# Low-rank weight loads on GpSimd's queue, and rotary halves swapped by ScalarE copies, in a two-layer hybrid encoder

## The chip, the cores and the metric

The kernel runs on one core of one Trainium2 chip. The metric is the device time of one execution in microseconds (us), as the median of several runs. The engines are TensorE (PE; its weight loads are shown as PEld), VectorE (DVE), ScalarE (ACT), GpSimd (POOL) and SyncE (SP). Each engine executes its instructions in order; where one waits, all behind it on that engine wait too. Transfers are issued by the queue of an engine (here always SP before the change) and carried by the core's 16 DMA engines.

## The reference

Two layers, on x of 256 tokens by 2048 channels in float32. Cut to what matters here:

```
for l in range(2):
    h = rms_norm(x, norm_g[l])
    proj = h @ w_in[l]                       # r, k, v, xw, xa | g_rw | q, k_at, v_at, g_at
    r, k, v, xw, xa = bidir_token_shift(...) # neighbours mixed in, xw and xa have 96 columns
    # group A, 16 heads of 64, one scan per direction d:
    w = -softplus(-(w0[d] + tanh(xw) @ decay_up[d])) - 0.5      # low rank: 96 -> 1024
    a = sigmoid(a0[d] + xa @ iclr_up[d])                        # low rank: 96 -> 1024
    y_rw = wkv_scan(...) both directions, normed, plus bonus * v
    # group B, 16 query heads on 4 key heads of 64, window of 128:
    q, k_at = rope(q), rope(k_at)            # t1*cos - t2*sin, t2*cos + t1*sin on halves of 32
    y_at = softmax over the band, with a sink logit, times v_at
    x = x + concat(y_rw * silu(g_rw), y_at * silu(g_at)) @ w_out[l]
out = rms_norm(x) * final_g
```

## The kernel before

Everything is held transposed: channels on the 128 partitions, the 256 tokens along the free dimension. A projection tile is 128 output columns. It is computed in one PSUM tile `pm` (two of them in rotation) by 16 steps over the 2048 input channels, and each step is three matmuls (lines 269 to 271): weights and activations are each split into a rounded part (`hi`, `XH`) and a rest (`lo`, `XL`), and hi*hi, hi*rest and rest*hi are added up.

The weights come as half tiles of 512 KB: `wload` (line 203) issues the load from SP into one of three `raw` buffers, and `wsplit` (lines 211 and 212) makes `hi` on ACT and `lo` on DVE, in two pieces of 512 columns each; two buffers of hi and lo are in rotation. The class `Stream` hands out the steps of all projections in a fixed order and starts a split one half tile ahead.

PE's order of work is written out by hand: the function `window` deals out 64 steps of projection in 14 slots and lets the generators of the scan (`scan_p`, `scan_i`, `scan_b`) or of the attention (`attend`) advance between slots. So the group A projections of head pair p run while earlier pairs are being scanned. The instructions of all other engines and queues are put in order by a scheduler that lists what is ready in its own estimate of time, by priority; this order is then fixed.

Per layer the projection order is: the two tiles of xw and xa; for each of 8 head pairs the tiles k, v, r and gate; v of the attention; two tiles of attention keys; eight of queries and eight of gates. The output projection has 16 tiles.

The places that the change touches:

- `ups` (lines 449 to 455), called at the first step of a pair's k tile. It loads the pair's columns of iclr_up (`iup`, 96 partitions of 2 x 128 numbers, tile `iu`) and of decay_up with the bias row w0 (`dup`, 97 partitions, tile `du`) into the two buffers of tag "g". The same two buffers serve the gate's `silu_evac` (lines 403 to 407), so a pair's loads wait until line 407 of the pair before.
- `value_evac` (line 457), one tile later, splits both into hi and rest: line 436 on ACT (`iuh`, `duh`), line 437 on DVE. `scan_p` uses them in matmuls (lines 617 to 619).
- `rope_evac` (lines 478 to 497), at the end of each of the two key tiles and eight query tiles of a layer. It copies `pm` to `raw` (tag "u") on ACT (line 487), loads `raw` into `rot` (tag "rrot") with neighbouring blocks of 32 partitions swapped, by four transfers from SP (line 489), and then multiplies and adds on DVE (lines 490 to 492); lines 494 and 495 split the result.
- POOL computes only the inverse square roots of norms: line 872 in `scan_b`, once per head pair, and line 190, once per layer and at the end.

Of the kernel before, what the change touches and what calls it, by code (L numbers as in the profile page):

```python
# [15 lines left out]
AF = mybir.ActivationFunctionType  # L16
ALU = mybir.AluOpType
# [111 lines left out]
def hybrid_trunk_kernel(ctx, tc, xT, wi, wv, wo, par, fing, dup, iup, sink, pos, cst, out):  # L129
    nc = tc.nc  # L130
    V, A, G, PE, SY = nc.vector, nc.scalar, nc.gpsimd, nc.tensor, nc.sync
# [18 lines left out]
    def st(tag, shape, dt=F32, bufs=1):  # L150
        return sp.tile([128, *shape], dt, tag=tag, name=tag, bufs=bufs)
# [230 lines left out]
    def queue_inputs(l):  # L382
# [66 lines left out]
        def ups(p, t):  # L449
            def begin():  # L450
                for n, src, rows in (("iu", iup, RANK), ("du", dup, RANK + 1)):
                    t[n] = st("g", [2, 128], bufs=2)
                    SY.dma_start(out=t[n][0:rows], in_=src[l, :, :, p * 128 : (p + 1) * 128].rearrange("d r c -> r d c"))

            return begin

# [21 lines left out]
        def rope_evac(place):  # L478
            def evac(pm):
                if not rope:  # L480
                    rope.extend((st("TW", [T]), st("XA", [T])))
                    V.tensor_tensor(rope[0], COS, L.norm.rb, op=ALU.mult)
                    V.tensor_tensor(rope[1], SIN, L.norm.rb, op=ALU.mult)
                CR, SR = rope
                raw = st("u", [T], bufs=2)
                rot = st("rrot", [T])
                A.activation(raw, pm, AF.Copy)
                for q in range(4):
                    SY.dma_start(out=rot[q * 32 : q * 32 + 32, :], in_=raw[(q ^ 1) * 32 : (q ^ 1) * 32 + 32, :])
                V.tensor_tensor(raw, raw, CR, op=ALU.mult)  # L490
                V.tensor_tensor(rot, rot, SR, op=ALU.mult)
                V.tensor_tensor(raw, raw, rot, op=ALU.add)
                hi, lo = place()
                A.activation(hi, raw, AF.Copy)
                V.tensor_tensor(lo, raw, hi.bitcast(F32), op=ALU.subtract)

            return evac
# [602 lines left out]
```

## Time and profile before

| | us |
|---|---|
| median of 3 runs | 1258.41 (1256.91 to 1259.39) |
| the profiled execution | 1254.45 |
| its span, first to last instruction | 1252.7 |
| PE busy | 1202.7 (96%) |
| PE weight load busy | 1126.2 (90%) |
| DVE busy | 947.1 (76%) |
| ACT busy | 735.6 (59%) |
| POOL busy | 18.5 (1%) |

The granted clock of TensorE, as a mean over the span, was 0.993 of full speed. Layer 0 runs to about 640 us, layer 1 after it.

How to read the rows. In the order of time a row is: start in us, duration in us, engine, line of the kernel, operation, output <- inputs by the program's names, count, and in brackets the time that the engine stood idle before it and what ended the idling. "SPq" is SP's queue, and L453 on it a DMA issue of line 453; several issues in a row are merged. A row of the waits is: who waited, for whom, then us in total, how many times, the longest. A row of a group is: line, engine, operation, shapes, count, busy us and mean ns of one. A row of the windows is: from:to, length, busy us of PE, PEld, DVE, ACT and POOL with instruction counts, granted clock of PE, mean share of the 16 DMA engines that was busy, GB/s.

### The profile page before, as it was taken

Reading aid. Unit: us, or ns where it says so; the run is one execution under the profiler, and the core shown is the slowest. Engines: PE = TensorE matmul, PEld = TensorE weight load, DVE = VectorE, ACT = ScalarE, POOL = GpSimd, SP = SyncE. Lnnn points to the kernel's source line nnn. Section 1 sums busy time; section 2 is a strip of 40 time slices with the busy share of each in tenths; the row PEclk is TensorE's granted clock in tenths of the full one; section 3 lists DMA queues with packets and bytes.
Section 4 is the critical chain, followed back from the end, with each engine's and each line's share of the span. In section 5 each row is a group of like instructions: output and inputs, shape, how many; then the busy total and the mean of one; then the engine's idle time right before and its main releaser. Section 6 shows DMA issues by size and latency. Waiting matters only on the chain.

```text
span 1252.7 us, 37475 instructions
## 1 busy us (share of the span) xinstructions
PE 1202.7 (96%) x15852; PEld 1126.2 (90%) x15852; DVE 947.1 (76%) x2113; ACT 735.6 (59%) x1838; POOL 18.5 (1%) x23
## 2 busy tenths in 40 slices
PE   7979999999999999999998999999999999999996
PEld 6979899999998988999998889999999888899996
DVE  7888878887886678856677878877887766786554
ACT  6655665665565466645555655665665555666553
POOL 0000000000000000000000000000000000000000
PEclk9999999999999999999999999999999999999998
DMA  6543223332323434366654333223322333345653
GB/s 245 163 136 120 92 92 122 100 96 95 120 86 96 131 109 144 123 219 230 210 188 142 126 125 103 92 92 125 103 92 86 116 108 129 126 143 168 213 192 119
DMA packets 60408, 166.67 MB, mean 133 GB/s; under 512 B 7728, under 2 KB 22736, under 8 KB 60240
## 3 DMA queue, kind: packets, MB, share of 16 engines
q1 hardware_dynamic: 60240, 164.27, 39.6%
q8 instruction: 124, 2.03, 0.7%
q14 instruction: 44, 0.36, 0.1%
HBM read 157.43 MB, written 4.19 MB: 129 GB/s over the span
## 4 chain that ended last, share of the span: by engine, by line
PE 66%; issue 15%; DVE 8%; ACT 6%; DMA 3%; SPq 1%; POOL 0%; POOLq 0%; DVEq 0%; ACTq 0%
PE pm L269 16%; PE pm L271 14%; PE pm L270 13%; PE pq L785 3%; PE pg L706 2%; DMA g<-dup 2%; DVE lo L212 2%; PE pd L796 2%; ACT suv L744 2%; PE pcc L831 2%; ACT AB L750 2%; PE pd L798 1%; PE py L840 1%; PE pcc L845 1%; ACT bt L739 1%
## 5 line engine op out<-in xcount | busy, mean ns | idle before, releaser
L269 PE MATMUL pm<-XH,hi 128*128 128x256 f32 x1664 | 499.9, 300 | 11.1 <-ACT XH L174 5.7
L211 ACT ACTIVATE hi<-raw 128x512 fp32r<-128x512 f32 x560 | 327.0, 623 | 272.6 <-PE pm L270 211.9
L271 PE MATMUL pm<-XH,lo 128*128 128x256 f32 x1664 | 470.5, 283 | 11.2 <-DVE lo L212 11.2
L270 PE MATMUL pm<-XL,hi 128*128 128x256 f32 x1664 | 469.6, 282 | 0.0
L212 DVE TENSOR_TENSOR lo<-raw,hi 128x512 fp32r<-128x512 f32 x560 | 369.7, 687 | 77.5 <-ACT hi L211 68.9
L269 PEld LDWEIGHTS pm<-XH,hi 128*128 128x128 f32 x1664 | 315.8, 190 | 24.8 <-ACT XH L174 6.0
L271 PEld LDWEIGHTS pm<-XH,lo 128*128 128x128 f32 x1664 | 316.0, 190 | 14.3 <-DVE lo L212 14.3
L270 PEld LDWEIGHTS pm<-XL,hi 128*128 128x128 f32 x1664 | 316.4, 190 | 1.5 <-DVE XL L175 0.7
L269 PE MATMUL pm<-MH,hi 128*128 128x256 f32 x512 | 144.5, 282 | 1.7 <-ACT hi L211 1.7
L271 PE MATMUL pm<-MH,lo 128*128 128x256 f32 x512 | 144.4, 282 | 0.4 <-DVE lo L212 0.4
L270 PE MATMUL pm<-ML,hi 128*128 128x256 f32 x512 | 144.1, 282 | 0.0
L269 PEld LDWEIGHTS pm<-MH,hi 128*128 128x128 f32 x512 | 97.1, 190 | 2.6 <-ACT hi L211 1.9
L271 PEld LDWEIGHTS pm<-MH,lo 128*128 128x128 f32 x512 | 97.1, 190 | 0.6 <-DVE lo L212 0.6
L270 PEld LDWEIGHTS pm<-ML,hi 128*128 128x128 f32 x512 | 97.2, 190 | 0.0
L785 PE MATMUL pq<-tv,AB 64*64 64x32 f16 x1536 | 43.8, 182 | 12.6 <-ACT AB L750 12.6
L850 ACT ACTIVATE suv<-pcc 64x128 f32<-64x128 f32 x128 | 34.4, 268 | 35.0 <-PE pcc L845 33.4
L785 PEld LDWEIGHTS <-AB 64*64 64x64 f16 x1536 | 34.4, 109 | 20.5 <-ACT AB L750 14.1
L752 DVE TENSOR_TENSOR AL<-ge,AB 64x512 f16<-64x512 f32 x32 | 22.0, 686 | 36.2 <-ACT AB L750 34.8
L799 DVE CAST_PREDICATED tv<-LV,pd 128x256 f16<-128x256 uint8 x80 | 34.4, 430 | 19.7 <-PE pd L798 18.8
L713 DVE TENSOR_TENSOR ge<-pg,C 128x512 f32<-128x512 f32 x64 | 41.3, 684 | 9.4 <-PE pg L706 9.4
L926 ACT ACTIVATE mv<-mv,mx 128x257 f32<-128x257 f32 x64 | 31.9, 500 | 23.2 <-DVE mx L923 23.2
L706 PE MATMUL pg<-mv,bk 64*128 64x128 f32 x512 | 37.2, 285 | 0.0
(230 smaller groups left out, 1863.9 us busy)
## 6 DMA issues: line engine op xcount, KB each, us to landing
raw<-wi SPq DMA_DIRECT2D x207, 512.0 KB
raw<-wo SPq DMA_DIRECT2D x64, 512.0 KB
raw<-wv SPq DMA_DIRECT2D x8, 512.0 KB
rrot<-u SPq DMA_DIRECT2D x80, 32.0 KB
vg<-xT SPq DMA_DIRECT2D x16, 128.0 KB
xd<-vg SPq DMA_DIRECT2D x16, 128.0 KB
vg<-xd SPq DMA_DIRECT2D x16, 128.0 KB
g<-dup SPq DMA_DIRECT2D x16, 97.0 KB
```

The lines of the kernel that those rows point to most:

```text
L211: A.activation(hi[:, q], raw[:, q], AF.Copy)
L212: V.tensor_tensor(lo[:, q], raw[:, q], hi[:, q].bitcast(F32), op=ALU.subtract)
L269: PE.matmul(pm, wh, rh[:, kk, :], start=(kk == 0), stop=False)
L270: PE.matmul(pm, wh, rl[:, kk, :], start=False, stop=False)
L271: PE.matmul(pm, wl, rh[:, kk, :], start=False, stop=(kk == 15))
L706: PE.matmul(pgs[h][:, c * 128 : (c + 1) * 128], BK[half[h], d, c, 1 - h : 3 - h, :].rearrange("p s j -> p (s j)"), MV[half[h], d, c].rearr ...
L713: V.tensor_tensor(GE[h][:, d].rearrange("p c s j -> p c (s j)"), pgs[h].rearrange("p (c x) -> p c x", c=NC), gm[d].unsqueeze(1).to_broadca ...
L744: A.activation(pick(SUV, half[1 - h], q * 128 + h * 64, [NC * 128, 2], [256, 2], [1, 64]), pts[h][half[q], 384:512].rearrange("p (b x) -> ...
L785: PE.matmul(narrow(pq, d, c, h), hq(AB, d, c, h), sub(TC, d, c, h, d * b), start=True, stop=True)
L799: V.copy_predicated(t_sub(TC), t_mask, flat4(pd))
L850: A.activation(here(h), pc[half[h], 1], AF.Copy)
L926: A.activation(Sc[:, h, q, 0:257], Sc[:, h, q, 0:257], AF.Exp, scale=0.125, bias=mx[:, q : q + 1], accum_out=den[:, q : q + 1])
```

## The change

It has two parts. The loads of the low-rank weights are issued from GpSimd's queue instead of SP's. And the swapped halves for the rotation are made by four ScalarE copies of 32 partitions each, straight from PSUM, instead of one ScalarE copy and four transfers; the first product on VectorE then reads PSUM too.

```
             def begin():
                 for n, src, rows in (("iu", iup, RANK), ("du", dup, RANK + 1)):
                     t[n] = st("g", [2, 128], bufs=2)
-                    SY.dma_start(out=t[n][0:rows], in_=src[l, :, :, p * 128 : (p + 1) * 128].rearrange("d r c -> r d c"))
+                    G.dma_start(out=t[n][0:rows], in_=src[l, :, :, p * 128 : (p + 1) * 128].rearrange("d r c -> r d c"))
...
                 raw = st("u", [T], bufs=2)
                 rot = st("rrot", [T])
-                A.activation(raw, pm, AF.Copy)
                 for q in range(4):
-                    SY.dma_start(out=rot[q * 32 : q * 32 + 32, :], in_=raw[(q ^ 1) * 32 : (q ^ 1) * 32 + 32, :])
-                V.tensor_tensor(raw, raw, CR, op=ALU.mult)
+                    A.activation(rot[q * 32 : q * 32 + 32, :], pm[(q ^ 1) * 32 : (q ^ 1) * 32 + 32, :], AF.Copy)
+                V.tensor_tensor(raw, pm, CR, op=ALU.mult)
                 V.tensor_tensor(rot, rot, SR, op=ALU.mult)
                 V.tensor_tensor(raw, raw, rot, op=ALU.add)
```

More of the change, by code (lines that the diff above doesn't have):

```diff
@@ L452, in begin @@
                     t[n] = st("g", [2, 128], bufs=2)
-                    SY.dma_start(out=t[n][0:rows], in_=src[l, :, :, p * 128 : (p + 1) * 128].rearrange("d r c -> r d c"))
+                    G.dma_start(out=t[n][0:rows], in_=src[l, :, :, p * 128 : (p + 1) * 128].rearrange("d r c -> r d c"))
             return begin
@@ L486, in evac @@
                 rot = st("rrot", [T])
-                A.activation(raw, pm, AF.Copy)
                 for q in range(4):
-                    SY.dma_start(out=rot[q * 32 : q * 32 + 32, :], in_=raw[(q ^ 1) * 32 : (q ^ 1) * 32 + 32, :])
-                V.tensor_tensor(raw, raw, CR, op=ALU.mult)
+                    A.activation(rot[q * 32 : q * 32 + 32, :], pm[(q ^ 1) * 32 : (q ^ 1) * 32 + 32, :], AF.Copy)
+                V.tensor_tensor(raw, pm, CR, op=ALU.mult)
                 V.tensor_tensor(rot, rot, SR, op=ALU.mult)
```

## The prediction

> **What bounds it now.** I read the page first (busy shares), then the idle gaps in PE's order of time, then the chain of waits, then the rows of the engines that PE waited for.
>
> ```profile
> span 1252.7 us, 37475 instructions
> PE 1202.7 (96%) x15852; PEld 1126.2 (90%) x15852; DVE 947.1 (76%) x2113; ACT 735.6 (59%) x1838; POOL 18.5 (1%) x23
> ```
>
> PE is busy 96% of the span, with a fixed amount of matmul, so only its 50 us of idle time, and stretches at a lower granted clock, can be won. PE's order of time shows where it idles; in brackets stand the idle time and what ended it.
>
> ```profile
> 65.49 0.38 PE L269 MATMUL pm<-XH,hi 128*128 128x256 f32 x1 [1.97 <-ACT hi L211]
> 69.52 0.38 PE L271 MATMUL pm<-XH,lo 128*128 128x256 f32 x1 [1.56 <-DVE lo L212]
> 75.51 0.39 PE L271 MATMUL pm<-XH,lo 128*128 128x256 f32 x1 [1.51 <-DVE lo L212]
> ...
> 352.31 0.42 PE L785 MATMUL pq<-tv,AB 64*64 64x32 f16 x15 [0.39 <-ACT AB L750]
> 398.79 0.61 PE L785 MATMUL pq<-tv,AB 64*64 64x32 f16 x15 [2.34 <-ACT AB L750]
> ...
> 558.55 0.38 PE L269 MATMUL pm<-MH,hi 128*128 128x256 f32 x1 [1.66 <-ACT hi L211]
> 559.43 0.58 PE L271 MATMUL pm<-MH,lo 128*128 128x256 f32 x1 [0.37 <-DVE lo L212]
> 678.54 0.38 PE L269 MATMUL pm<-XH,hi 128*128 128x256 f32 x1 [1.36 <-ACT hi L211]
> 682.57 0.39 PE L271 MATMUL pm<-XH,lo 128*128 128x256 f32 x1 [1.57 <-DVE lo L212]
> 688.56 0.38 PE L271 MATMUL pm<-XH,lo 128*128 128x256 f32 x1 [1.45 <-DVE lo L212]
> 1001.01 0.34 PE L811 MATMUL pn<-tt,q 64*64 64x64 f16 x10 [0.91 <-DVE q L807]
> 1010.94 0.42 PE L785 MATMUL pq<-tv,AB 64*64 64x32 f16 x15 [1.03 <-ACT AB L750]
> ```
>
> Three groups (65 to 76, 558, 678 to 689) wait for the weight split (hi on ACT, lo on DVE). A fourth (398.79, 1001 and 1010) is a scan step; in a pair without rotation the same wait is 0.39 (352.31). The question is what held ACT and DVE. The waits give it, then their rows at those places:
>
> ```profile
> ACT duh L436 <- DMA g<-dup: 10.4, 4, 4.4
> DVE u L490 <- DMA rrot<-u: 9.8, 11, 2.1
> ```
>
> ```profile
> 56.89 0.30 SPq L453 DMA_DIRECT2D g<-dup  x1
> 64.50 0.42 ACT L436 ACTIVATE duh<-g 97x256 fp32r<-97x256 f32 x1 [2.21 <-DMA g<-dup]
> 549.23 0.42 SPq L453 DMA_DIRECT2D g<-iup  x1
> 549.69 0.38 SPq L453 DMA_DIRECT2D g<-dup  x1
> 552.75 0.42 ACT L436 ACTIVATE iuh<-g 96x256 fp32r<-96x256 f32 x1 [0.42 <-DMA g<-iup]
> 557.57 0.42 ACT L436 ACTIVATE duh<-g 97x256 fp32r<-97x256 f32 x1 [4.40 <-DMA g<-dup]
> 669.54 0.30 SPq L453 DMA_DIRECT2D g<-dup  x1
> 677.55 0.42 ACT L436 ACTIVATE duh<-g 97x256 fp32r<-97x256 f32 x1 [2.57 <-DMA g<-dup]
> ```
>
> Each of the three groups follows an ACT that stands, in order, at duh until dup has landed: 7.6, 7.9 and 8.0 us after its issue. The split of the next weights is queued behind it. iup, a partition smaller, landed in 3.5 (549.23 to 552.75). The windows say why dup is late, and what an idle PE costs on top:
>
> ```profile
> 90.50:93.50 3.00, 1.50 (x25) 1.24 (x24) 0.87 (x2) 2.92 (x7) 0.00 (x0) 1.00 0.07 22
> ...
> 398.00:404.00 6.00, 5.21 (x60) 4.86 (x61) 4.33 (x10) 4.44 (x10) 0.00 (x0) 0.72 0.00 0
> 558.00:564.00 6.00, 5.08 (x28) 4.87 (x29) 4.14 (x9) 3.13 (x7) 0.00 (x0) 0.72 0.64 202
> ```
>
> From 90.5 to 93.5, with a dup in flight, the DMA share is 0.07, about one engine of 16, at 22 GB/s: its 97 KB crawl through one engine. After two of the PE gaps the granted clock averages 0.72 over 6 us: (1 - 0.72) x 6 = 1.7 us lost at each.
>
> **The change, part by part: the low-rank loads.** 32 issues (16 iup, 16 dup) leave SP, whose weight loads then no longer queue behind them, and go to POOL's queue. They still wait for the release of the two "g" buffers, so their issue time hardly moves. What queues behind them on POOL is the power of the scan's norm (and the layer's):
>
> ```profile
> 169.33 0.29 DVE L768 COPY tt<-EYE 128x512 f16<-128x512 f16 x1
> 169.82 0.30 SPq L453 DMA_DIRECT2D g<-dup  x1
> 180.48 0.41 ACT L436 ACTIVATE duh<-g 97x256 fp32r<-97x256 f32 x1
> 205.64 1.01 POOL L872 TENSOR_TENSOR yv<-yv,mhalf 128x4 f32<-128x4 f32 x1 [42.95 <-DVE yv L871]
> ```
>
> The power comes 36 us after the pair's loads and POOL idles 42.95 before it: cost nothing. In such a settled pair dup has 180.48 - 169.82 = 10.7 us until it is asked for, so a faster landing gains nothing there; the gain lies at the three places above.
>
> No row shows a load on POOL's queue. Bounds of dup's landing: 3.5 us (iup, 549.23), if it spreads over the engines; 8.0 (669.54), if it doesn't; above that only if POOL is slow to make it. It no longer stands behind weight loads in one queue, but POOL takes 1.01 us even for 128x4 elements, and iup goes first. I take 3.5 + 2 x 1.0 = 5.5, nearer the iup row, since dup differs from it by one partition. That is 2.1 (56.89), 2.4 (549.69) and 2.5 us (669.54) earlier.
>
> The rule for this is in the Trainium skill, DMA: Bandwidth & Descriptors, "Why a DMA increments its semaphore by 16 and not by 1": the engines used are the largest number up to 16 that divides the slowest dimension, which for 97 partitions is one. The 0.07 agrees. It names an exception: from GpSimd some plain copies use all 16, with the partitions dealt out. No run yet shows whether this load is one; with the exception the sum is mine, without it rival A.
>
> - Layer 0, second pair: PE's gaps are 1.97 + 1.56 + 1.51 = 5.0. ACT is released 2.1 us earlier; DVE, saturated after it, gets that time too. Gain 2.1 (0 to 5.0).
> - Layer 0, output projection: 1.66 + 0.37 of gap and 1.7 of clock. ACT's wait of 4.40 shrinks to 2.0, and 2.4 us earlier covers both gaps, so the clock has no reason to fall. Gain 3.7 (0 to 3.7).
> - Layer 1, second pair: gaps of 1.36 + 1.57 + 1.45 = 4.4, ACT released 2.5 earlier. Gain 2.4 (0 to 4.4).
> - Kernel start: the first pair's loads wait for nothing and may go out beside the first loads of x.
>
> ```profile
> 6.00:14.00 8.00, 6.64 (x24) 5.29 (x24) 6.78 (x17) 7.49 (x18) 0.00 (x0) 1.00 1.00 371
> 29.19 0.42 ACT L436 ACTIVATE duh<-g 97x256 fp32r<-97x256 f32 x1 [1.26 <-DMA g<-dup]
> ```
>
> At 371 GB/s their 193 KB push x back by 0.5; a wait of 1.26 goes. I count 0 (0.5 lost to 1.3 won).
>
> **The rotation.** Per tile of q or k: out go one ACT copy, four SP issues, four transfers; in come four ACT copies of 32 partitions from PSUM. VectorE's first product then reads PSUM.
>
> ```profile
> 387.55 0.37 ACT L487 ACTIVATE u<-pm 128x256 f32<-128x256 f32 x1
> 387.94 3.80 SPq L489 DMA_DIRECT2D rrot<-u  x4
> 393.15 0.43 DVE L490 TENSOR_TENSOR u<-u,TW 128x256 f32<-128x256 f32 x1 [2.09 <-DMA rrot<-u]
> ...
> L744 ACT ACTIVATE suv<-pt 64x256 f32<-64x256 f32 x64 | 24.2, 379 | 0.7
> L487 ACT ACTIVATE u<-pm 128x256 f32<-128x256 f32 x20 | 7.4, 369 | 0.1
> L394 DVE TENSOR_TENSOR u<-pm,rb 128x256 f32<-128x256 f32 x52 | 21.4, 414 | 9.8 <-PE pm L271 9.8
> ...
> 430.00:520.00 90.00, 88.81 (x907) 80.91 (x906) 70.36 (x216) 57.02 (x169) 1.01 (x1) 1.00 0.40 132
> ```
>
> From the ACT copy to DVE's product it now takes 5.6 us, and DVE, in order, stands idle 2.09 of it; the scan's work is queued behind. Half the partitions (L744) cost 379 ns where 128 cost 369, so 32 will not be cheaper: 4 x 0.38 - 0.37 = 1.15 us more of ACT per tile, 23 us in 20 tiles; latency falls to about 1.6 us. The product from PSUM costs what it did: 0.43 now (393.15), and the token shift reads pm at 414 ns (L394). pm is held some 2 us longer, until DVE has read it too; the next tile's 48 matmuls go to the other bank and, at the page's mean of 1202.7 / 15852 = 0.076 us, which the small ones pull down, take 3.6 or more. If that cover were gone, PE would wait for those 2. SP loses 80 issues, 3.80 us at each tile, and its weight loads start that much sooner; no PE gap above ends with such a load, so it counts 0.
>
> - Layer 0, second k tile: gap 2.34 back to 0.39 (1.95), and 1.7 of clock. Gain 3.6 (0 to 3.6).
> - Layer 1, same place: 0.91, and 1.03 back to 0.39. I take 1.4 of the 1.55.
> - The 16 q tiles: ACT is 57.0 of 90 us busy between 430 and 520, so most of the 1.15 lies beside other work; but the copies come just when the next split is due. I take 0.15 each of 0 to 1.15: loss 2.4 (0 to 18.4).
>
> **Sum:** 2.1 + 3.7 + 2.4 + 3.6 + 1.4 - 2.4 = 10.8 us won. The profiled execution took 1254.45 (span 1252.7), 4.0 under the median 1258.41; from the former 1243.7, on the scale of the median 1258.4 - 10.8 = 1247.6.
>
> **Rivals.** About 2.5 us (0.2%) is what a measurement here tells from no change.
>
> A. dup stays on one engine, and lands as late as now. Left is the rotation: 3.6 + 1.4 - 2.4 = 2.6, so 1255.8. For it: 0.07 now. Against: iup's 3.5 in the same form. The page's general rule speaks for it.
>
> B. ScalarE becomes late in the attention stage: 0.6 us shown per q tile, 9.6 in all instead of 2.4. Won remain 3.6, so 1254.8. For it: the split's queue; against: ACT's idle third.
>
> C. Slower: POOL makes the descriptors so slowly that dup lands later than today. Place: the same three waits of ACT. Each us beyond 7.9 costs 3; with 2.6 won by the rotation it decides (2.5 us slower) from a landing of 7.9 + 5.1 / 3 = 9.6 us. At 10.7, where the settled pairs begin to wait too, it is 3 x 2.8 - 2.6 = 5.8 slower: 1264.2. For it: 1.01 us for 512 elements on POOL. Against: nothing else runs there. The Trainium skill, SBUF — State Buffer, "SBUF: two separate sides", speaks for C: GpSimd can't write descriptors while VectorE runs a two-port copy. By the rows such a copy (L768) stands beside the issue, but it lasts 0.29 us, and is over 0.2 us before 169.82.
>
> **Chances.** My forecast 0.60, A 0.14, B 0.13, C 0.09, a reordering of ACT or DVE that costs more than all this 0.04. Faster by over 0.2%: 0.59 + 0.08 of A + 0.09 of B = 0.76. Within: 0.01 + 0.06 + 0.03 = 0.10, slower 0.01 + 0.09 + 0.04 = 0.14. The range: all upper bounds give 5.0 + 3.7 + 4.4 + 3.6 + 1.55 + 1.3 = 19.5, so 1239; up to 1259 it takes in A and B and leaves out C and the reordering.
>
> **What would show it.** Right: dup's transfer spread over the engines (no stretch at a DMA share of 0.07), ACT's wait for dup near zero, no clock of 0.72 after the output projection's start or the second k tile, no wait of L490 for a DMA. Wrong: duh waiting for DMA longer than 10.4 us in sum (C), or as long (A); PE waiting for the split after each group of four copies (B); PE gaps that move elsewhere.

## The result, and the profile after

The changed kernel took 1288.81 us in the median of 4 runs (1287.32 to 1289.56), beside 1257.66 for the kernel before on the same chip: a ratio of 1.0245, 95% interval 1.0228 to 1.0263. It is 31 us slower. The forecast was 10.8 us faster, and 1288.8 lies far above the range. In the profiled execution the changed kernel took 1288.49 us, 34.0 more than the 1254.45 of before.

The page of the kernel after, its first lines and its lines on the two loads (kind, count, KB each, median us from issue to landing):

```profile
span 1286.7 us, 37383 instructions
PE 1211.9 (94%) x15852; PEld 1134.9 (88%) x15852; DVE 947.7 (74%) x2113; ACT 761.6 (59%) x1898; POOL 76.0 (6%) x55
...
g<-dup POOLq DMA_DIRECT2D x16, 97.0 KB, 9.4
g<-iup POOLq DMA_DIRECT2D x16, 96.0 KB, 3.2
```

PE's idle time, span less busy, went from 50.0 to 74.8 us; the other 9.2 us of the longer span are PE busy for longer with the same 15852 matmuls. So two things are to be found: 24.8 us in which PE waited, and 9.2 us in which the same matmuls took longer. iup lands after 3.2 us, much as it did (3.5 in the prediction's rows); dup, one partition larger, in 9.4. The waits, and the groups of the two issues on POOL, show who felt it:

```profile
ACT duh L436 <- DMA g<-dup: 37.9, 4, 12.3
DVE u L489 <- ACT rrot L488: 15.3, 20, 1.5
```

```profile
L453 POOL DMA_DIRECT2D g<-dup x16 | 46.4, 2902 | 0.9
L453 POOL DMA_DIRECT2D g<-iup x16 | 10.8, 676 | 337.1 <-DVE vg L407 336.2 <-POOLq L1091 0.9
```

ACT's wait for dup is 37.9 us where it was 10.4. Issuing dup holds POOL for 2.90 us each time, issuing iup for 0.68. (From the rotation on, the line numbers of the changed kernel are lower by one.) A window with a dup in flight, the last three columns being granted clock, DMA share and GB/s:

```profile
76.00:79.00 3.00, 0.52 (x5) 0.31 (x3) 0.00 (x0) 0.00 (x0) 0.00 (x0) 1.00 0.09 23
```

The DMA share is 0.09, little over one engine of 16, as it was before. PE's order of time after shows where that reached PE:

```profile
19.04 0.58 PE L269 MATMUL pm<-XH,hi 128*128 128x256 f32 x1 [19.04 <-ACT XH L174]
...
82.33 0.58 PE L269 MATMUL pm<-XH,hi 128*128 128x256 f32 x1 [5.81 <-ACT hi L211]
83.68 0.58 PE L271 MATMUL pm<-XH,lo 128*128 128x256 f32 x1 [0.55 <-DVE lo L212]
86.98 0.58 PE L271 MATMUL pm<-XH,lo 128*128 128x256 f32 x1 [0.37 <-DVE lo L212]
93.80 0.38 PE L271 MATMUL pm<-XH,lo 128*128 128x256 f32 x1 [1.04 <-DVE lo L212]
...
571.05 0.56 PE L269 MATMUL pm<-MH,hi 128*128 128x256 f32 x1 [5.11 <-ACT hi L211]
705.82 0.58 PE L269 MATMUL pm<-XH,hi 128*128 128x256 f32 x1 [5.15 <-ACT hi L211]
707.17 0.58 PE L271 MATMUL pm<-XH,lo 128*128 128x256 f32 x1 [0.55 <-DVE lo L212]
710.47 0.58 PE L271 MATMUL pm<-XH,lo 128*128 128x256 f32 x1 [0.37 <-DVE lo L212]
716.50 0.38 PE L271 MATMUL pm<-XH,lo 128*128 128x256 f32 x1 [1.23 <-DVE lo L212]
```

The same three places as before, each with a first gap of over 5 us where it was 1.4 to 2.0, and a new one: the very first matmul comes at 19.04 us. Before, it came here:

```profile
5.72 0.58 PE L269 MATMUL pm<-XH,hi 128*128 128x256 f32 x1 [5.72 <-ACT XH L174]
```

So of the 24.8 us of idle time, 13.3 are at the start, and the three places hold 2.7 (5.81 + 0.55 + 0.37 + 1.04 against 5.04), 3.1 (5.11 against 2.03) and 2.9 (7.30 against 4.38): 22.0 together. The rest, 2.8, lies in small gaps. The windows after the first and the third place give the clock:

```profile
80.00:89.00 9.00, 5.75 (x23) 5.16 (x24) 8.45 (x16) 6.69 (x16) 0.00 (x0) 0.50 0.12 36
704.00:711.00 7.00, 4.26 (x16) 3.67 (x17) 6.94 (x15) 6.17 (x15) 0.00 (x0) 0.52 0.00 0
```

After such a gap PE runs at half its clock for most of 7 to 9 us: its rows at 82.33 to 86.98 take 0.58 us, that at 93.80 0.38. PE was busy 5.75 us at 0.50 and 4.26 us at 0.52, which costs it some 2.9 and 2.0 us.

That is about half of the 9.2 us. The output projection adds little: there the clock fell before too (0.72 over 6 us from 558), and after the change it is 0.57 over 4 us from 571, 1.7 us lost in both. The remainder lies behind gaps that are no longer than those of before: the granted clock is 0.66 over 5 us from 509, 0.52 over 7 us from 735 and 0.57 over 4 us from 1134, behind gaps of 1.40, 1.50 and 1.38 us. The first and the last of these come with the rotation (e2_rot_only below). At the start, rows of 0.4 to 0.6 us stand in both kernels, until about 20 us before and 25 us after; there the clock column reads 1.00, and the rows tell more than it does.

Why the start? ACT's order of time in the first 20 us, and POOL's:

```profile
5.44 0.42 ACT L436 ACTIVATE iuh<-g 96x256 fp32r<-96x256 f32 x1 [1.39 <-DMA g<-iup]
18.17 0.42 ACT L436 ACTIVATE duh<-g 97x256 fp32r<-97x256 f32 x1 [12.32 <-DMA g<-dup]
18.50 0.89 ACT L174 ACTIVATE XH<-X,G 128x256 fp32r<-128x256 f32 x2
...
1.31 0.80 POOL L453 DMA_DIRECT2D g<-iup  x1 [0.87 <-POOLq L1091]
2.12 2.90 POOL L453 DMA_DIRECT2D g<-dup  x1
```

On POOL's queue nothing stands ahead of the first pair's loads, so they go out at once. Before, dup went out on SP at 19.73 us, behind loads of weights:

```profile
19.73 0.35 SPq L453 DMA_DIRECT2D g<-dup  x1
```

The scheduler then put the splits iuh and duh ahead of the split of x (XH) in ACT's fixed order; before, duh came at 29.19 us, long after. dup takes until 18 us to land, and XH, for which PE waits, is queued behind it. Why this one takes 16 us, where the median is 9.4, no run shows.

### The profile page after: what moved, and what is told of

Read it like the earlier page. It is cut to its first block, busy times and chain, and to the rows that moved or that the text cites. A ratio compares the mean times of both kernels' runs of the same rounds, so it can differ in the third digit from the quotient of the medians.

```text
span 1286.7 us, 37383 instructions
## 1 busy us (share of the span) xinstructions
PE 1211.9 (94%) x15852; PEld 1134.9 (88%) x15852; DVE 947.7 (74%) x2113; ACT 761.6 (59%) x1898; POOL 76.0 (6%) x55
## 3 DMA queue, kind: packets, MB, share of 16 engines
q0 software_dynamic: 7424, 3.35, 1.3%
q8 instruction: 124, 2.03, 0.6%
## 4 chain that ended last, share of the span: by engine, by line
PE 66%; issue 17%; ACT 7%; DVE 7%; DMA 2%; POOL 1%; POOLq 0%; DVEq 0%; ACTq 0%
PE pm L269 16%; PE pm L271 14%; PE pm L270 13%; PE pg L705 2%; PE pq L784 2%; DMA g<-dup 2%; PE pd L795 2%; ACT suv L743 2%; PE pcc L830 2%; ACT AB L749 2%; PE pd L797 1%; PE py L839 1%; DVE lo L212 1%; PE pcc L844 1%; ACT bt L738 1%
## 5 line engine op out<-in xcount | busy, mean ns | idle before, releaser
L269 PEld LDWEIGHTS pm<-XH,hi 128*128 128x128 f32 x1664 | 319.3, 192 | 48.4 <-ACT XH L174 19.0
L271 PEld LDWEIGHTS pm<-XH,lo 128*128 128x128 f32 x1664 | 319.6, 192 | 12.5 <-DVE lo L212 12.5
L270 PEld LDWEIGHTS pm<-XL,hi 128*128 128x128 f32 x1664 | 319.8, 192 | 1.4 <-DVE XL L175 0.6
L784 PE MATMUL pq<-tv,AB 64*64 64x32 f16 x1536 | 43.8, 182 | 11.9 <-ACT AB L749 11.5
L871 POOL TENSOR_TENSOR yv<-yv,mhalf 128x4 f32<-128x4 f32 x16 | 16.3, 1022 | 564.2 <-DVE yv L870 564.2
L453 POOL DMA_DIRECT2D g<-dup x16 | 46.4, 2902 | 0.9
```

The costliest lines, as they stand in the source:

```text
L269: PE.matmul(pm, wh, rh[:, kk, :], start=(kk == 0), stop=False)
L270: PE.matmul(pm, wh, rl[:, kk, :], start=False, stop=False)
L271: PE.matmul(pm, wl, rh[:, kk, :], start=False, stop=(kk == 15))
L453: G.dma_start(out=t[n][0:rows], in_=src[l, :, :, p * 128 : (p + 1) * 128].rearrange("d r c -> r d c"))
L784: PE.matmul(narrow(pq, d, c, h), hq(AB, d, c, h), sub(TC, d, c, h, d * b), start=True, stop=True)
```

## The experiments

Theory 1, formed from these rows: dup's 97 partitions still travel on one engine, and POOL needs 2.9 us to issue them; dup therefore lands later than before, ACT stands at duh in order, and at the start it does so ahead of everything. The rivals: the copies of the rotation cost the time (rival B of the prediction), or POOL's queue is slow whatever it loads. In what follows each kernel's edit is shown against the kernel before or the changed one.

**One half alone: the loads (e1_loads_only).** Against the kernel before:

```
-                    SY.dma_start(out=t[n][0:rows], in_=src[l, :, :, p * 128 : (p + 1) * 128].rearrange("d r c -> r d c"))
+                    G.dma_start(out=t[n][0:rows], in_=src[l, :, :, p * 128 : (p + 1) * 128].rearrange("d r c -> r d c"))
```

> The loads on GpSimd's queue, the rotation as before. Theory 1 (dup of 97 partitions stays on one DMA engine, takes GpSimd 2.9 us to issue, lands 9 to 16 us later, and ACT stands at duh in order, 12.3 us of it at the start): this half alone gives the whole loss, 1290 us (1283 to 1296), ACT's wait for dup 36 to 40 us in sum, first matmul near 19 us. Rival B (the four copies on ACT cost it): 1258 us (1254 to 1264).

Measured: 1287.94 us, ratio 1.0248 (1.0221 to 1.0276). Its waits and PE's first matmul:

```profile
ACT duh L436 <- DMA g<-dup: 38.7, 4, 13.5
```

```profile
19.96 0.58 PE L269 MATMUL pm<-XH,hi 128*128 128x256 f32 x1 [19.96 <-ACT XH L174]
```

The loads alone give the whole loss, and the same wait. Rival B falls.

**The other half alone: the rotation (e2_rot_only).** The diff is the second part of the change.

> The rotation by ACT copies, the loads on SP as before. Theory 1: 1256 us (1252 to 1260), the second k tile's wait down from 2.34 to 1.2 us in layer 0, about 0.5 to 1.4 us lost at some q tiles. Rival B: the copies cost most of the 31 us, 1275 us or more.

Measured: 1257.85 us, ratio 0.9997 (0.9982 to 1.0013): no difference. PE's order of time at the second k tile of layer 0 and at the q tile concerned, and ACT's before the latter:

```profile
398.76 0.42 PE L784 MATMUL pq<-tv,AB 64*64 64x32 f16 x15 [1.16 <-ACT AB L749]
489.94 0.38 PE L269 MATMUL pm<-XH,hi 128*128 128x256 f32 x1 [1.38 <-ACT hi L211]
...
486.72 1.53 ACT L488 ACTIVATE rrot<-pm 32x256 f32<-32x256 f32 x4
488.28 0.60 ACT L940 ACTIVATE pp<-ppt 128x512 f32<-128x512 f32 x1
488.77 0.59 ACT L940 ACTIVATE ip<-ppt 128x512 f32<-128x512 f32 x1
489.25 0.63 ACT L211 ACTIVATE hi<-raw 128x512 fp32r<-128x512 f32 x1
```

The k tile's wait falls from 2.34 to 1.16 us, and at a q tile PE now waits 1.38 us for hi, since four copies, 1.53 us together, stand in ACT's order ahead of it, with two copies of line 940 between. In each layer two waits of 0.48 and 0.52 us at line 795 are new besides (2.0 us in sum). The clock after the k tile stays at 1.00 (398 to 404 us), where it was 0.72 before, but falls to 0.72 over 6 us in three other places (from 680, 706.3 and 1014 us), and PE's busy time is 1207.7 us, 5.0 more than before. It is a gain in some places and a loss in others.

**The shape, on POOL (e3_pool_96_1).** Against the changed kernel, dup in two transfers, of 96 rows and of 1:

```
-                    G.dma_start(out=t[n][0:rows], in_=src[l, :, :, p * 128 : (p + 1) * 128].rearrange("d r c -> r d c"))
+                    G.dma_start(out=t[n][0:RANK], in_=src[l, :, 0:RANK, p * 128 : (p + 1) * 128].rearrange("d r c -> r d c"))
+                    if rows > RANK:
+                        G.dma_start(out=t[n][RANK:rows], in_=src[l, :, RANK:rows, p * 128 : (p + 1) * 128].rearrange("d r c -> r d c"))
```

> As the changed kernel, all on GpSimd's queue, but dup goes as 96 rows and 1 row in two transfers. Theory 1: each issue takes GpSimd 0.7 us, dup lands after about 4 us, ACT's wait for it falls from 37.9 to under 10 us, what is left of it is at the start (first matmul at 7 to 9 us); 1254 us (1246 to 1262). Rival (GpSimd's queue is slow for any load, the shape doesn't matter): dup lands after 9 us or more still, 1280 us or more.

Measured: 1260.68 us, ratio 1.0017 (1.0002 to 1.0031). Four views of it: its issues of dup on POOL, their landing, ACT's wait and PE's start:

```profile
L453 POOL DMA_DIRECT2D g<-dup x16 | 10.2, 637 | 0.0
```

```profile
g<-dup POOLq DMA_DIRECT2D x16, 96.0 KB, 4.2
```

```profile
ACT duh L436 <- DMA g<-dup: 7.9, 4, 3.5
```

```profile
9.27 0.58 PE L269 MATMUL pm<-XH,hi 128*128 128x256 f32 x1 [9.27 <-ACT XH L174]
```

One row fewer in the transfer: 0.64 us to issue instead of 2.90, landing after 4.2 instead of 9.4, and all but 2 of the 31 us are back. POOL's queue isn't slow for any load. 1260.7 is some 7 us above the middle of what I expected. Its first matmul is still 3.6 us late, and its PE busy is 1208.0 us, 5.3 above that of before; as e2_rot_only has 1207.7 with all loads on SP, the queue is not needed for this part.

**The number of engines (e8_pool_95_2).** As e3_pool_96_1, with 95 and 2 rows.

> As the changed kernel, but dup goes as 95 rows and 2 rows. Theory 1 (it is the number of engines that counts, and 95 rows go over 5 of them): the 95 rows land after 4.5 to 7 us, between the 4.2 of 96 rows and the 9.4 of 97, their issue takes GpSimd between 0.7 and 2.9 us, ACT's wait for dup is 8 to 20 us in sum, 1267 us (1258 to 1276). Rival (any count but a multiple of 16 is as slow as 97): issue near 2.9 us, landing after 9 us, 1285 us or more.

Measured: 1262.40 us, ratio 1.0030 (1.0015 to 1.0044). The same four views:

```profile
L454 POOL DMA_DIRECT2D g<-dup x16 | 16.4, 1024 | 0.0
```

```profile
g<-dup POOLq DMA_DIRECT2D x16, 95.0 KB, 4.6
```

```profile
ACT duh L436 <- DMA g<-dup: 12.9, 4, 5.1
```

```profile
11.35 0.58 PE L269 MATMUL pm<-XH,hi 128*128 128x256 f32 x1 [11.35 <-ACT XH L174]
```

For 96, 95 and 97 rows the issue takes 0.64, 1.02 and 2.90 us, the landing 4.2, 4.6 and 9.4, and PE starts at 9.3, 11.4 and 19.0. The order is not that of the sizes but that of the largest divisor up to 16: 16, 5 and 1. That is the general rule quoted in the prediction from the Trainium skill, DMA: Bandwidth & Descriptors, "Why a DMA increments its semaphore by 16 and not by 1"; these rows agree with it on GpSimd's queue, and 97 rows, at a share of 0.09, are not its exception. That 95 rows used 5 engines is the rule's number; the rows show the order alone.

**The shape, on SP (e4_sp_96_1).** The kernel before with dup as 96 rows and 1, all on SP.

> The kernel before, on SP, but dup goes as 96 rows and 1 row. Theory 1 (the shape makes dup slow, on SP too): dup lands after about 4 us instead of 7.6 to 8.0, ACT's wait for it falls from 10.4 us to under 3, the gaps of PE at the second pairs and the output projection of layer 0 shrink: 1249 us (1243 to 1254). Rival (dup is slow for the weight loads that it shares the engines with): no change, 1258 us.

Measured: 1252.31 us, ratio 0.9951 (0.9936 to 0.9967), 6.3 us faster. ACT's rows at the second pair of layer 0:

```profile
59.91 0.42 ACT L436 ACTIVATE iuh<-g 96x256 fp32r<-96x256 f32 x1 [1.66 <-DMA g<-iup]
60.95 0.41 ACT L436 ACTIVATE duh<-g 97x256 fp32r<-97x256 f32 x1
61.25 0.62 ACT L211 ACTIVATE hi<-raw 128x512 fp32r<-128x512 f32 x1
```

duh no longer waits for a transfer there, nor anywhere else in this kernel, and of PE's gaps those of 1.97, 1.66 and 1.36 are gone or under 0.45. The later gaps of the two second pairs stay (1.62 and 1.50, 1.62 and 1.49), so they did not hang on duh. The shape made dup late on SP too.

**The start (e6_first_sp).** The changed kernel, with the first pair's loads of layer 0 on SP:

```
-                    G.dma_start(
+                    (SY if l == 0 and p == 0 else G).dma_start(
```

> As the changed kernel, but the first pair of layer 0 loads through SP. Theory 1 (on GpSimd's idle queue these loads go out first of all, ACT's order puts their split ahead of the split of x, and PE starts 13.3 us late): first matmul back at 6 us, 1274 us (1269 to 1278); the other 16 us of the loss stay, at the second pairs and at the output projection of layer 0. Rival (the start is late for another reason, such as the x loads): 1289 us.

Measured: 1274.24 us, ratio 1.0109 (1.0087 to 1.0130).

```profile
6.67 0.58 PE L269 MATMUL pm<-XH,hi 128*128 128x256 f32 x1 [6.67 <-ACT XH L174]
...
70.15 0.58 PE L269 MATMUL pm<-XH,hi 128*128 128x256 f32 x1 [5.78 <-ACT hi L211]
...
557.19 0.58 PE L269 MATMUL pm<-MH,hi 128*128 128x256 f32 x1 [5.00 <-ACT hi L211]
692.00 0.58 PE L269 MATMUL pm<-XH,hi 128*128 128x256 f32 x1 [5.17 <-ACT hi L211]
```

Two issues of 32 put back, and the loss against the kernel before falls from 31.2 to 15.4 us (1274.24 - 1258.81; 11.0 to 16.4 by the interval); the three gaps of 5 us stay. Between the two profiled executions the start is worth 14.0 us (1288.49 - 1274.45). The start is thus about half of the loss.

**Both mended, still on POOL (e9_pool_96_1_first_sp).** The edits of e3_pool_96_1 and e6_first_sp together.

> As the changed kernel, with both causes taken away: dup as 96 rows and 1 row, and the first pair of layer 0 loads through SP; all other pairs on GpSimd's queue. Theory 1 (with the shape and the start mended, GpSimd's queue is no worse than SP's): 1252 us (1248 to 1256), like e5_sp_96_1_rot, first matmul at 6 us. Rival (GpSimd's queue costs something of its own): 1257 us or more.

Measured: 1252.51 us, ratio 0.9949 (0.9927 to 0.9972), first matmul at 5.50 us. With the shape and the start mended, GpSimd's queue costs nothing that can be measured beside SP's, and gains nothing.

**The version that beats both, and the key tiles (e5_sp_96_1_rot, e7_sp_96_1_krot).** e5 is e4_sp_96_1 with the whole rotation of the change, e7 with the rotation's copies at the four key tiles alone.

> Loads on SP as 96 rows and 1 row, and the rotation by ACT copies. Theory 1 (the two halves of the change are independent, the rotation alone gave 0.03% and the 96 + 1 rows 0.5%): 1252 us (1248 to 1256), like e4_sp_96_1. If the rotation's gain at the second k tile was only hidden by the late dup: 1249 or less.

> As e4_sp_96_1, with the rotation by ACT copies in the four key tiles alone; the sixteen query tiles keep their transfers. Theory (the rotation's zero is a gain at the second k tile, 1.2 us of wait and 1.7 us of clock, cancelled by a loss at a q tile in each layer, where PE then waits 1.4 us for hi): 1249.5 us (1246 to 1252), 2 to 3 us under e4_sp_96_1 and e5_sp_96_1_rot. Rival (neither part matters): 1252 us.

Measured: e5 1251.47 us, ratio 0.9928 (0.9903 to 0.9953); e7 1251.71, ratio 0.9933 (0.9914 to 0.9952). e5 is 7.3 us under the kernel before and 37 under the changed one. Between e4, e5 and e7 the intervals overlap; that the key tiles alone gain 2 to 3 us did not show, though the wait at the second k tile is 1.14 us in both e5 and e7 and 2.35 in e4. That theory is not supported, nor is a gain of 1 us excluded.

## Why the prediction was wrong, point by point

- **The landing of dup, 5.5 us: the step that failed.** It measured 9.4. Its place in the argument was right: three times ACT stands at duh, and PE runs dry behind it. But I took a landing "nearer the iup row, since dup differs from it by one partition", and that one partition is what counts (e3, e8). Two parts were wrong. The transfer was taken to spread over the engines, against the 0.07 that I had quoted and the general rule; it did not. And POOL's work was taken at 1.0 us for each load, from a row of arithmetic on 512 elements; it is 0.68 for iup and 2.90 for dup. 9.4 - 2.9 leaves 6.5 us after the issue, near the 7.6 to 8.0 that SP's dup took with its issue of 0.30 to 0.38: on SP's queue and on POOL's the transfer is about as slow, and POOL adds its issue. The premise of rival A was right, but not its landing "as late as now"; and the sign named for rival C, a wait for dup longer than 10.4 us in sum, is what the trace shows.
- **The kernel start, counted 0 (0.5 lost to 1.3 won), failed too: it cost about 15 us** (15.7 by 31.2 - 15.4, 14.0 between the profiled executions; e6). I saw that the first pair's loads "wait for nothing", but priced their bytes beside x, and not the order. That the issue time hardly moves holds for 15 of the 16 pairs (336.2 us of waiting for L407), and not for the first, whose buffers are free and which was held on SP by what stood ahead of it in the queue. Moved to an empty queue it went out 17.6 us earlier (19.73 - 2.12), and with it two instructions of another engine, ACT, moved ahead of x.
- **Rival C was the right mechanism, at 0.09, with a price too low.** It named the place, the slow issue and a landing from 9.6 us on. From issue to duh the three places now take 9.5, 10.5 and 9.8 us (79.84 - 70.35, 570.07 - 559.52, 703.32 - 693.54) instead of 7.6, 7.9 and 8.0: 6.3 us later in sum, and by rival C's rule of 1 us each, less the 2.6 of the rotation, 3.7 slower. Measured without the start: 15.4. The gaps grew by 8.7, and the rival left out the half clock after a gap of 5 us. PE's busy time in e6_first_sp is 1210.6 us, 7.9 more than before. Not all of it belongs to these gaps: with the rotation alone it is 5.0 more (e2), with the loads alone, which have the gaps, 4.6 more (1207.3, e1), so the clock behind the gaps makes some 3 to 5 us. These rows, of the changed kernel, carry the landings:

```profile
70.35 2.90 POOL L453 DMA_DIRECT2D g<-dup  x1
...
79.84 0.42 ACT L436 ACTIVATE duh<-g 97x256 fp32r<-97x256 f32 x1 [9.74 <-DMA g<-dup]
...
559.52 2.90 POOL L453 DMA_DIRECT2D g<-dup  x1
570.07 0.42 ACT L436 ACTIVATE duh<-g 97x256 fp32r<-97x256 f32 x1 [6.79 <-DMA g<-dup]
...
693.54 2.91 POOL L453 DMA_DIRECT2D g<-dup  x1
703.32 0.42 ACT L436 ACTIVATE duh<-g 97x256 fp32r<-97x256 f32 x1 [9.09 <-DMA g<-dup]
```

- **What three earlier landings are worth: about right.** The 8.2 us of the three places were for a dup that is no longer late. e4_sp_96_1, which makes it so on SP, won 6.3 (4.2 to 8.1 by its interval). In its profile the three places hold 4.9 us of gap less (6.6 instead of 11.5), and after the output projection's start the clock stays at 1.00 (555 to 565 us), 1.7 won: 6.6 in sum (4.9 + 1.7). The two profiled executions differ by 2.5 us only: that of before lies 4.0 under its median, and some other gaps of e4 are longer (2.69 at 14.32 us, 1.82 at 431.37 and 1.71 at 1041.14). The gain was there; GpSimd's queue was not what it needed.
- **The rotation, 2.6 us won: the run says 0.8 won, between 2.3 won and 1.6 lost** (e2). The copies cost what I took: 375 ns, and ACT is busy 26 us longer (23 expected). The product from PSUM is 425 ns against 424. The two terms that were mis-sized: the k tile's wait fell from 2.34 to 1.16, not to 0.39, and one q tile in each layer makes PE wait 1.38 us, where I had spread 0.15 over sixteen. Layer 1's two waits of 0.91 and 1.03 became one of 1.14, 0.8 won where I took 1.4. The clock after the second k tile was won as forecast, and lost again elsewhere. DVE's wait did not go: 9.8 us for the transfers became 15.3 us for the copies (L489 in the waits above), a change that I had not followed.
- **POOL's power, costed at nothing: right.** DVE waited 16.3 us for it in sum after, 14.2 before, and no gap of PE ends there.
- **The lock-out of GpSimd** that I cited for rival C from the Trainium skill, SBUF — State Buffer, "SBUF: two separate sides", isn't seen: all 16 issues of dup took 2.90 to 2.91 us, in stretches where DVE was busy 0.50 us of 2.8 (from 70.40) and 2.23 of 2.8 (from 105.90) alike. But what DVE executed beside these issues were products, sums and differences (TENSOR_TENSOR), no copy, so what a two-port copy would do to them no run here shows.

## What to carry to other kernels

Before a load is moved to another queue, ask why it is slow: here its 97 partitions were, on either queue, and 96 + 1 on the queue where it stood won most of what the move was to win. A load that is moved to an empty queue may go out earlier than it should, and the instructions that wait for it, placed in the fixed order of another engine, then stand ahead of the work that everything hangs on; look at the first instance, whose buffers are free. And price a PE gap with the clock behind it.

## What the runs showed of the hardware that was not expected

An issue on GpSimd's queue depends on the shape far more than on the size: 0.64, 1.02 and 2.90 us for 96, 95 and 97 partitions of 1 KB each. The number of packets on that queue goes the same way, 2048, 2816 and 7424 in the whole execution for 3.17, 3.19 and 3.35 MB (iup and the rows split off included); that the packets are what makes the issue long is not shown. And the lower clock does not follow from the gap alone. The same scan step, after the same PE gap of 1.50 us in layer 1, ran at full clock in the kernel before and at 0.72 over 6 us with the rotation alone:

```profile
705.50:711.50 6.00, 5.79 (x74) 5.46 (x76) 4.81 (x10) 5.19 (x12) 0.00 (x0) 1.00 0.28 96
```

```profile
706.30:712.30 6.00, 5.83 (x60) 5.54 (x61) 3.41 (x7) 3.87 (x10) 0.00 (x0) 0.72 0.31 97
```

The first row is of the kernel before, the second of e2_rot_only. (1 - 0.72) x 6 is 1.7 us, the size of each of the two drops that the prediction priced. The Trainium skill, TensorE: Matmul & The Clock Gate, "Part 1: The HAM clock gate (the "warmup" mystery)", says that the clock is full or half, and is set by free-running windows of about 3.4 us; half of 3.4 is 1.7, so the row agrees with the size. The same section has the half clock come after an idle window of that length, which a gap of 1.50 us is not, so it does not tell when such a gap ends in a drop, and no run here does. The runs do show that lost clock comes and goes in one and the same kernel: the 26 runs of the kernel before beside which e1 to e4 stand had mean clocks from 0.985 to 0.994 and took 1253.86 to 1262.43 us. Gains of 2 us are at the edge of what one profile can tell.
